# The position bias's rows to DRAM: one transfer from a borrowed tile, or eight from a tile of their own

## The chip, the cores and the metric

The kernel runs on one core of one Trainium2 chip. Its time is the device time of one execution, in microseconds (us). Engines are named as in the profile: PE multiplies, PEld loads its weights, ACT and DVE do elementwise work, POOL and SP here mostly issue DMA transfers. A transfer is cut into packets that run on the core's 16 DMA engines, whoever issued it.

## The reference

Two layers of a decoder trunk on 512 tokens of width 2048, in float32. Each layer normalises its input, projects it once, and runs two groups of attention heads on the result: eight heads of differential attention (two softmax maps a head) and eight heads of latent attention (low-rank queries, keys and values, a shared rotary key). Both are gated, joined and projected back.

Only the differential heads use the position bias: 32 buckets by 8 heads, one table for both layers.

```python
dist = (start + jnp.arange(BLOCK_Q, dtype=jnp.int32))[:, None] - kpos[None, :]
bias = jnp.transpose(table[_t5_bucket(dist)], (2, 0, 1))
s = jnp.where((dist >= 0)[None, None, None], s + bias[None, None], NEG_INF)
```

So the bias of a head is a function of the distance alone: one row of 640 numbers holds all of it (640 covers 512 keys and 128 query rows), and each query row reads that row at another offset.

## The kernel before

Activations lie feature-major, 128 features on the partitions and 512 tokens along a row. Every float32 operand of a matmul is split into a high and a low part, and each product is three matmuls (`mm3`). The weights come from DRAM as 290 blocks of 128 x 1024 numbers (512 KB, a few of half that). `WStream` handles them: SP issues the load of a block into one of two `raw` buffers (line 75), ACT casts it to `whi` (line 94), DVE subtracts to get `wlo` (line 95), and PE uses the pair. There are two buffers of each kind. The load of block i+2 can be issued only when DVE has finished with block i, so at most two loads are under way.

PE, SP and POOL execute in the order in which the program is written; the order on ACT and DVE is chosen by a scheduler. `run_jobs` sets the written order: jobs are generators of matmuls with a `yield` after every few, and a list of steps says after which yield each small piece of work is written down. A step sets a place in the order of the program. It makes an engine wait only if one of its instructions needs something that is not there yet.

The first layer begins with the compressed query (`job_kouter`), the rotary key (`job_kr`) and the compressed keys and values (four `job_proj`). In step 34 of these, `bias_rows` (line 823) multiplies the table with a one-hot matrix: PE writes an 8 x 640 result, DVE copies it to `tv` (line 832), and POOL issues one transfer that writes each of the eight rows 128 times to the DRAM tensor `brow` (line 833). The source pattern has 8 partitions, then a step of 0 with a count of 128, then 640 numbers. `tv` borrows the one buffer of tag `pth`, which the heads' transposed probabilities use later (`new_pt`).

After that come the eight units of latent attention (in the first layer and then in the second), each with its own jobs and `mla_steps`, and then the eight units of differential attention. At the start of each of these, `load_bias` (line 838) reads one head's bias from `brow` with a row step of 639, which gives each partition its own offset.

## Time and profile before

| | us |
|---|---|
| median of 3 runs | 1840.79 (1840.78 to 1840.84) |
| profiled execution, its own time | 1841.41 |
| its span in the trace | 1839.6 |
| PE busy | 1795.7 (98% of the span) |
| DVE busy | 1021.9 (56%) |
| ACT busy | 878.8 (48%) |
| POOL busy | 38.0 (2%) |

How to read it: the span is what the trace covers, and the execution's own time has 1.8 us more around it. PE is busy nearly all the time, so what is left to gain or lose lies in the few stretches in which PE stands still or runs at a lower clock, and in the work itself.

## The change

The 8 x 640 result gets a tile of its own, so the buffer of tag `pth` is no longer borrowed. The single transfer is removed from `bias_rows`. In its place the new function `bias_out` issues the transfer of one head's row, and a step at place 2 of each of the first layer's eight units of latent attention calls it. The number of bytes is the same.

```diff
-        tv = t_([NH, 640], F32, "pth", 1)
+        tv = sb.tile([NH, 640], F32, name="tv")
         for o, n in ((0, 512), (512, 128)):
             ps = p_("tp", 2)
             nc.tensor.matmul(ps[:NH, :n], tab, st["onehot"][:, o:o + n], start=True, stop=True)
             nc.vector.tensor_copy(out=tv[:, o:o + n], in_=ps[:NH, :n])
-        nc.gpsimd.dma_start(out=brow, in_=bass.AP(tensor=tv.tensor, offset=tv.offset, ap=[list(tv.ap[0]), [0, P], [1, 640]]))
+        st["tv"] = tv
+
+    def bias_out(hd):
+
+        row = st["tv"][hd:hd + 1, :]
+        nc.gpsimd.dma_start(out=brow[hd:hd + 1], in_=bass.AP(tensor=row.tensor, offset=row.offset, ap=[list(row.ap[0]), [0, P], [1, 640]]))
...
-            add(jobs, mla_steps(h, keep(8 + h), after(MLA_AT if h else FIRST_AT, sum(n for n, _ in jobs))))
+            add(jobs, mla_steps(h, keep(8 + h), after(MLA_AT if h else FIRST_AT, sum(n for n, _ in jobs))),
+                [(2, lambda h=h: bias_out(h))] if l == 0 else [])
```

The order of POOL's instructions from the start of the program, before the change, with the semaphores that each waits for (`DVE` counts DVE's instructions, `DMASW` the landings of POOL's own transfers, `DMAHW` those of SP's):

```order
masks.py:197 MEMSET ident 128x128
masks.py:199 ISA
masks.py:199 AFFINE_SELECT ident<-ident 128x128 [waits Pool_49]
L833 DMA brow<-pth_748 1024x1x640 [waits DVE_49]
L838 DMA cs_2933<-brow 128x512 [waits DMAHW6_49,DMASW0_49,DVE_49]
L838 DMA cs_2935<-brow 128x512 [waits DMAHW7_49,DVE_49]
```

And of the changed kernel, where line 838 is the transfer in `bias_out` and line 843 the load in `load_bias`:

```order
masks.py:197 MEMSET ident 128x128
masks.py:199 ISA
masks.py:199 AFFINE_SELECT ident<-ident 128x128 [waits Pool_49]
L838 DMA brow<-tv 128x1x640 [waits DVE_49]
L838 DMA brow<-tv 128x1x640 x7
L843 DMA cs_2940<-brow 128x512 [waits DMAHW6_49,DMASW0_49,DVE_49]
L843 DMA cs_2942<-brow 128x512 [waits DMAHW7_49,DMASW1_49,DVE_49]
```

One issue of 1024 rows has become eight of 128 rows that follow each other; the first waits for DVE, the other seven wait for nothing.

On ACT, in the first unit of latent attention, before the change (line 678 casts the transposed probabilities to `pth`, line 434 the values):

```order
L719 ACTIVATE sa_1139<-sa_1139,m_1140 128x256
L434 CAST v_1090<-pacc_1086 128x512
L434 CAST v_1090<-po_1087 128x512
L434 CAST v_1090<-pacc_1088 128x512
L434 CAST v_1090<-pacc_1089 128x512
L94 CAST whi_1208<-raw_1145 128x1024
```

The same place in the changed kernel:

```order
L678 CAST pth_1157<-ptp_1159 128x128
L719 ACTIVATE sa_1139<-sa_1139,m_1140 128x256
L434 CAST v_1089<-pacc_1085 128x512
L434 CAST v_1089<-po_1086 128x512
L678 CAST pth_1157<-ptp_1179 128x2x128
L434 CAST v_1089<-pacc_1087 128x512
L434 CAST v_1089<-pacc_1088 128x512
L94 CAST whi_1208<-raw_1145 128x1024
```

The first two casts to `pth` have moved ahead of the values' casts; before the change they stood some ten instructions later, behind a wait for the transfer of `brow`. DVE's subtractions that follow them (line 679) move likewise. SP's order is unchanged, and PE's too.

## Rows read from the trace of the kernel before

**Rows 1.** The page: its first line, and three DMA issues (KB each, us to landing).

```profile
span 1839.6 us, 21822 instructions
...
raw<-in_blocks_dram SPq DMA_DIRECT2D x282, 512.0 KB, 3.5
...
brow<-pth POOLq DMA_DIRECT2D x1, 2560.0 KB, 56.6
...
xres<-tmp POOLq DMA_DIRECT2D x8, 256.0 KB, 2.3
```

**Rows 2.** Waits of PE from 80 to 150 us: total, times, longest.

```profile
PE ptp L312 <- ACT sa L307: 15.8, 1, 15.8
PE pacc L319 <- ACT whi L94: 11.5, 1, 11.5
PE pacc L321 <- DVE wlo L95: 0.4, 1, 0.4
```

**Rows 3.** The chain of waits from 88 to 146 us: start, us, what.

```profile
89.14 23.86 DMA raw<-in_blocks_dram
113.09 1.05 ACT whi L94
114.17 1.23 DVE wlo L95
115.42 23.81 DMA raw<-in_blocks_dram
139.33 1.05 ACT whi L94
140.41 1.23 DVE wlo L95
142.94 0.80 PE ptp L312
```

**Rows 4.** Busy time of engines in four stretches, then granted clock, DMA share, GB/s.

```profile
102.70:114.10 11.40, 0.00 (x0) 0.00 (x0) 0.00 (x0) 1.01 (x2) 0.00 (x0) 0.60 0.49 76
114.20:118.60 4.40, 4.36 (x9) 2.97 (x10) 1.79 (x2) 0.47 (x1) 0.00 (x0) 0.50 0.73 146
127.20:142.80 15.60, 0.00 (x0) 0.00 (x0) 1.83 (x2) 2.10 (x3) 0.00 (x0) 0.66 0.50 75
143.00:149.30 6.30, 6.30 (x14) 4.69 (x15) 4.14 (x6) 5.53 (x10) 0.00 (x0) 0.50 0.16 58
```

**Rows 5.** PE in order of time, before and after the first standstill: start, us.

```profile
101.81 0.39 PE L319 MATMUL pacc<-x,whi 128*128 128x512 f32 x1
102.03 0.39 PE L320 MATMUL pacc<-x,whi 128*128 128x512 f32 x1
...
116.47 0.63 PE L320 MATMUL pacc<-x,whi 128*128 128x512 f32 x1
116.89 0.63 PE L321 MATMUL pacc<-x,wlo 128*128 128x512 f32 x1
```

**Rows 6.** POOL in order of time from 80 to 360 us.

```profile
87.50 1.23 POOL L833 DMA_DIRECT2D brow<-pth  x1 [86.20 <-DVE pth L832]
317.83 1.12 POOL L838 DMA_DIRECT2D cs<-brow  x2 [229.09 <-DVE tmp L578]
356.19 0.54 POOL L838 DMA_DIRECT2D cs<-brow  x1 [37.24 <-DVE m L663]
```

**Rows 7.** DMA queues from 98.5 to 104 us: packets, MB, share of 16 engines.

```profile
q0 software_dynamic: 52, 0.27, 47.4%
```

**Rows 8.** DMA queues from 105 to 111 us.

```profile
q0 software_dynamic: 55, 0.28, 40.4%
q1 hardware_dynamic: 56, 0.23, 9.3%
```

**Rows 9.** DMA queues from 432 to 434 us, one block's load alone.

```profile
q1 hardware_dynamic: 139, 0.52, 76.5%
```

**Rows 10.** Loads of blocks issued from 85 to 146 us.

```profile
DMA to landing us min/median/max: 3.3/21.2/26.8
```

**Rows 11.** ACT in order of time: casts of weight blocks.

```profile
91.58 1.05 ACT L94 CAST whi<-raw 128x1024 fp32r<-128x1024 f32 x1 [3.06 <-PE pacc L320]
113.09 1.04 ACT L94 CAST whi<-raw 128x1024 fp32r<-128x1024 f32 x1 [20.46 <-DMA raw<-in_blocks_dram]
120.79 1.05 ACT L94 CAST whi<-raw 128x1024 fp32r<-128x1024 f32 x1 [6.12 <-DMA raw<-in_blocks_dram]
139.33 1.04 ACT L94 CAST whi<-raw 128x1024 fp32r<-128x1024 f32 x1 [17.49 <-DMA raw<-in_blocks_dram]
```

**Rows 12.** Instructions on `pth` from 100 to 200 us: the casts (ns, starts).

```profile
L678 ACT CAST pth<-ptp x6: 255/378/587, 180.4 to 198.7; 128x128 fp32r<-128x128 f32 x2, 128x256 fp32r<-128x256 f32 x2, 128x384 fp32r<-128x384 f32 x1, 128x512 fp32r<-128x512 f32 x1
```

**Rows 13.** Waits of PE from 150 to 450 us.

```profile
PE ptp L672 <- DVE ptl L679: 0.4, 1, 0.4
```

## What the change will do to the time

> **What bounds the kernel now.** I read the page first: PE is the bound, so I looked for the places where PE stands still. Of the waits of PE, three lie between 80 and 150 us and make 27.7 us: 11.5, 15.8 and 0.4 [rows 2]. The chain of waits says what stands behind the two long ones: a load of a weight block that took 23.9 us from issue to landing, and a second one of 23.8 us [rows 3]; ACT's casts at 113.1, 120.8 and 139.3 us all waited for such loads, where the one at 91.6 still waited for PE [rows 11]. Over the whole run such a load of 512 KB takes 3.5 us in the median [rows 1]. The only other thing under way is the transfer that writes the bias rows: 2560 KB, issued at 87.50 us, landed 56.6 us later, at 144.1 [rows 1, 6]. Loads issued in that time took up to 26.8 us, and the one issued as it ended took 3.3 again [rows 10].

> The standstills also cost clock. [...] At 0.50 a matmul starts every 0.42 to 0.43 us, at full clock every 0.22 to 0.23 [rows 5], so 23 matmuls lost some 0.2 us each: 4.6 us. In all the bias transfer costs the kernel 27.7 + 4.6 = 32.3 us. This is the most that any placing of it can win.

> **What the change does to the transfer.** It does not spread it. POOL executes in the order written, and a step only sets a place in that order. In the changed program the eight issues stand directly behind each other, the first waits for DVE's copy and the other seven for nothing. POOL is idle from 88.7 to 317.8 us [rows 6], so nothing else there holds them apart. An issue of 128 rows keeps POOL 0.54 us against 1.23 for the 1024 rows [rows 6]: eight make 4.3 us, and all are issued from 87.5 to about 91.8 us. I cost POOL's added 3.1 us at nothing: its next work comes at 317.8. So the same 2560 KB meet the same loads, and the question is how fast they move and which engines they keep.

> How fast they move now, from a stretch with no load in it: 52 packets in 5.5 us, 0.27 MB, 47.4% of 16 engines [rows 7]. That is 7.6 engines at work, so eight, one for each source row; 0.27 MB / 5.5 us = 49 GB/s; and 0.474 x 16 x 5.5 / 52 = 0.80 us for a packet of 0.27 MB / 52 = 5.2 KB (two rows of 2560 B). Where a load runs between them, its packets of 4 KB take 0.093 x 16 x 6 / 56 = 0.16 us, 25.7 GB/s on one engine [rows 8]. At that rate 5.12 KB would take 0.199 us; the bias packets take 4.03 times as long, as if four engines took turns at something that passes what one engine can move. The same rows show that it is not the engines that are full: with 9.3% given to the load, the bias still moved 55 packets in 6 us, 9.2 a us against 9.5, and each took only 0.404 x 16 x 6 / 55 = 0.71 us. So the eight rows have two such bottlenecks between them, each 25.7 GB/s, 51 together; this I take to lie on the reading side, four neighbouring partitions to one.

> [...]

> After the change each transfer reads one partition 128 times. **Which engines** carry it is not in the trace of before. A transfer of 128 rows runs on all 16: a load alone kept 76.5% of them busy in 2 us [rows 9]. One whose source had 8 partitions ran on eight. The new one has one partition and 128 repeats. The bounds are one engine and sixteen; I take sixteen, since both its sides count 128 rows, as the load does. [...]

> With sixteen engines at one bottleneck of 25.7 GB/s, 2.62 MB need 102 us instead of the 53.4 us at 49 GB/s. Adding the 3 us around it (56.6 - 53.4), the bias ends at about 87.5 + 3 + 102 = 192.5 us instead of 144.1. Rows 0 to 3 go through one bottleneck first and rows 4 to 7 through the other after them, since the transfers stand in line on the same engines.

> **What PE gets meanwhile.** A packet now takes 16 x 0.199 = 3.2 us on every engine. Of a load, each engine has 128 / 16 = 8 packets. Now a load takes 23.9 - 3.5 = 20.4 us longer, about 25 bias packets of 0.80 us, 8 of them in turn with its own and some 17 ahead of them. After the change an engine has 32 bias packets in all. The load issued at 89.14 finds those of three or four transfers ahead (12 to 16) and takes turns with 8 more: 20 to 24 packets, so it lands at 89 + 2 + 64 to 77 = 155 to 168, not at 113. The next (issued at 93.92) takes turns with the following 8 and lands near 183. The third can only be issued when the first is split; it lands with the end of the bias, about 192.5, not at 139.2. In the chain of before PE starts again 142.94 - 139.23 = 3.7 us after that landing [rows 3], so at 196 instead of 142.9: +53. The lower end is plain turn-taking with nothing ahead (8 x 3.2 us for each load): landings at 116, 142, 168 and 193, PE waiting for the fourth then and one block of work (24 matmuls of 0.227, 5.4 us) further than in the other case: +47. Lower clock is lost in either case after two or three standstills, as now, give or take 3 us. The upper end: both loads under way stay behind the whole bias to 192.5, so PE restarts at 194 with two blocks still to do (7.6 us with the low clock, 5.4 us without) and is at the third block at 207 instead of 142.9, with no standstill before it (-2.8 us): +61. I take +49, between the two that share turns.

> **The rest of the change.** The first two casts to `pth` and their subtractions stand earlier, since they no longer wait for the bias. They ran at 180 us [rows 12], after the transfer had landed at 144.1, so that wait had ended anyway. What may go is the one wait of PE for a subtraction, 0.4 us [rows 13]; what may come is a delay of a weight cast by two casts of 0.26 and 0.38 us: -0.4 to +0.6, taken as 0. A small reordering on DVE in the first differential unit is of the same size. If the bias lasts to 192.5, the borrowed tile would have held these casts at 180 back; with a tile of its own it does not, so this part of the change is a cover and no gain.

> **Sum.** 1841.4 + 49 = 1890.4; the profiled execution lies 0.6 above the median of 1840.8, so 1890. The likeliest case's own range is 1870 to 1912: +45 to +61, and some more at either end for a bottleneck that passes 5% more or 10% less (102 us x 0.1 = 10).

> **The rivals.**
> - One engine carries all eight transfers (faster). It would have the bottleneck to itself, 0.199 us a packet, for 102 us. A load's packets there wait 25 x 0.199 = 5.0 us, so it lands after 8.5 us. The load issued at 89.14 was needed when PE ran dry at 102.7 less 1.2 us for the cast [rows 3, 4], so 12 us are to spare and PE never stops: 1841.4 - 32.3 = 1809, up to 1818 if a few loads with less room come late. For it: a source with 8 partitions ran on eight engines, and this one has one. Against it: the 128 repeats on both sides.
> - The 49 GB/s belong to the transfer's queue or to all eight rows, and sixteen engines or eight change nothing in the sum: it ends at 144 as before. The first load lands at about 125 instead of 113 (a packet takes 1.6 us on 16 engines), and what PE loses there it gets back at the third, whose load now lands before it is needed: 1838 to 1848. Against it: the factor of 4.03 fits a count of four.
> - Each engine has its own 6.4 GB/s on such rows (5.12 KB / 0.80 us), and sixteen make 102 GB/s: the bias ends at 116, the second standstill of 15.8 us and its 2.8 us of clock go, 1822. Against it: the packets of 0.71 us [rows 8].
> - One partition can be read at 6.4 GB/s only: 410 us of bias, some 350 us slower. Against it: a transfer of 256 KB out of 128 partitions lands after 2.3 us, 16 KB an engine, over 7.1 GB/s each [rows 1].

> **How the numbers follow.** The likeliest case 0.66; one engine 0.13; the sum unchanged 0.11; 6.4 GB/s an engine 0.05; far slower, by this or another way, 0.05. For 8 times in 10 the range goes from 1818 to 1912: the first case, the unchanged sum, 6.4 GB/s an engine, and the edge of one engine. About 0.2% (3.7 us) can be told from no change. Faster: 0.13 + 0.05 and 0.02 of the unchanged sum, 0.20. Within: 0.07. Slower: 0.66 + 0.05 + 0.02 = 0.73.

> **What the profile of the changed kernel would show.** POOL: eight issues of about 0.54 us from 87.5 to 92 us; were they 20 us or more apart, the first step is wrong. DMA: in the stretch without loads 16 engines near full and about 26 GB/s; half of them and 49 GB/s, or one engine (6% and 26 GB/s), means a rival. Landing of the last bias row near 192 us. PE: a standstill of 50 to 65 us from 102.7, and one or two shorter ones before 196; none at all would mean that one engine carries it. From 200 us on nothing should differ by more than 1 us.

## The result, and the profile after

The changed kernel took 1890.15 us (median of four runs, 1887.34 to 1890.85) against 1840.78 of before (1840.64 to 1840.84), measured beside it: a ratio of 1.0266, interval 1.0251 to 1.0282. The execution that was profiled is the lowest of the four, 1887.34 us.

The page of the kernel after: its span, PE busy in 40 slices, and the line of the bias transfers (KB each, us to landing), to be read against [rows 1].

```profile
span 1885.6 us, 21827 instructions
...
PE   9922999999999999999999999999999999999997
...
brow<-tv POOLq DMA_DIRECT2D x8, 320.0 KB, 54.6
```

A slice is 47 us, so nearly all of the damage lies between 94 and 189 us. POOL in order of time from 80 to 360 us (start, us, what, how often) shows that the eight transfers were not spread:

```profile
87.07 4.28 POOL L838 DMA_DIRECT2D brow<-tv  x8 [85.77 <-DVE tv L832]
```

The same line's landings, all eight: 87.1 + 14.4 = 101.5 us for the first, 90.8 + 91.6 = 182.4 for the last, where the one transfer of before had landed at 144.1.

```profile
L838 POOL DMA_DIRECT2D brow<-tv x8: 522/524/663, 87.1 to 90.8; - x8
...
DMA to landing us min/median/max: 14.4/54.6/91.6
```

The DMA queues from 96 to 136 us (packets, MB, share of 16 engines; POOL's queue, then SP's), which answer [rows 7, 8]:

```profile
q0 software_dynamic: 263, 1.09, 90.6%
q1 hardware_dynamic: 176, 0.66, 4.0%
```

All 16 engines are kept by the bias, and together they move 1.09 MB in 40 us, 27 GB/s, where eight moved 49 before. A busy engine here is one that is held up: in experiment 3 the same queue moves 262 GB/s at a share of 73.6%. What the loads beside it pay stands in the chain of waits from 88 to 188 us, as in [rows 3]:

```profile
88.71 47.74 DMA raw<-in_blocks_dram
136.55 1.05 ACT whi L94
137.63 1.24 DVE wlo L95
138.88 44.81 DMA raw<-in_blocks_dram
183.80 1.05 ACT whi L94
184.87 1.23 DVE wlo L95
...
187.40 0.79 PE ptp L312
```

47.7 and 44.8 us for a load that took 23.9 and 23.8 before, and PE starts again at 187.40, not at 142.94. The load between these two, issued at 93.5 us, took longest. Loads of blocks issued from 85 to 160 us, to be read against [rows 10]:

```profile
DMA to landing us min/median/max: 3.5/38.5/59.8
```

The waits of PE from 80 to 700 us (total, times, longest), as in [rows 2, 13]:

```profile
PE pacc L319 <- ACT whi L94: 44.5, 2, 35.4
PE ptp L312 <- ACT sa L307: 26.3, 1, 26.3
PE ps L754 <- DVE m L663: 2.4, 1, 2.4
```

The first line holds two standstills, 35.4 and 9.1 us. And the stretches, as in [rows 4] (busy time of PE, PEld, DVE, ACT and POOL, granted clock, DMA share, GB/s): the longest standstill, and what follows each of the three.

```profile
102.30:137.50 35.20, 0.00 (x0) 0.00 (x0) 0.00 (x0) 0.95 (x1) 0.00 (x0) 0.57 0.99 52
137.70:141.50 3.80, 3.76 (x8) 2.56 (x9) 1.75 (x2) 0.43 (x1) 0.00 (x0) 0.50 0.89 43
...
154.60:158.60 4.00, 3.96 (x9) 2.66 (x10) 1.74 (x2) 0.00 (x0) 0.00 (x0) 0.50 0.86 24
...
187.40:192.70 5.30, 5.30 (x12) 3.90 (x13) 3.14 (x5) 4.55 (x8) 0.00 (x0) 0.50 0.11 42
```

After each of the three standstills PE runs 8, 9 and 12 matmuls at a granted clock of 0.50, 29 in all against 9 + 14 = 23 before [rows 4].

The difference of the two profiled executions, 1887.34 - 1841.41 = 45.9 us, comes out of these rows: standstills 35.4 + 9.1 + 26.3 = 70.8 against 27.7, +43.1; six more matmuls at 0.50, 0.2 us each [rows 5], +1.2; the new wait at L754, +2.4; a start 0.4 us earlier (POOL's issue at 87.07, not 87.50) and the wait of 0.4 at L672 that is gone, -0.8. Sum: +45.9. The medians lie 49.4 apart: the profiled execution of after is the fastest of its four and lies 2.8 below their median, while that of before lies 0.6 above its own. What makes the other executions of after some 3 us longer no trace here shows.

## The experiments

The theory: what holds the loads up is the reading of the bias rows. Few partitions are read through one bottleneck of some 26 GB/s (25.7 by the estimate from [rows 8], 27 measured in the kernel after), and the engines that carry them are held up with it. After the change all sixteen stand at one such bottleneck at a time. Rivals: the tile, the queue, the number of bytes written, the number of engines.

**1. The tile alone** (before, with the new tile and the single transfer).

```diff
-        tv = t_([NH, 640], F32, "pth", 1)
+        tv = sb.tile([NH, 640], F32, name="tv")
```

> One transfer of eight rows as before the change, but from a tile of its own. Theory (the loss comes from eight transfers that each read one partition): 1840.8, within 1 us of before, the transfer lands after 56 to 57 us and PE's standstills stay 11.5 and 15.8 us. Rival (the tile of its own, or the reordering of the casts that it brings, costs the time): 1880 or more.

1840.11 us against 1840.66, ratio 0.9997 (0.9988 to 1.0006). The waits of PE and the landing of the bias are those of before:

```profile
PE ptp L312 <- ACT sa L307: 15.8, 1, 15.8
PE pacc L319 <- ACT whi L94: 11.5, 1, 11.5
...
DMA to landing us min/median/max: 56.5/56.5/56.5
```

The tile, with the reordering of the casts that it brings, costs and gives nothing; the 49 us belong to the eight transfers and the steps that issue them.

**2. Eight rows from partitions four apart** (before, with the table's columns repeated four times, so that a matmul makes 32 rows; the one transfer reads partitions 0, 4, ... 28).

```diff
...
+        wide = st["wide"]
+        nc.vector.tensor_copy(out=wide.rearrange("k (h r) -> k h r", r=4), in_=bass.AP(tensor=tab.tensor, offset=tab.offset, ap=[list(tab.ap[0]), [1, NH], [0, 4]]))
-        tv = t_([NH, 640], F32, "pth", 1)
+        tv = t_([4 * NH, 640], F32, "pth", 1)
...
-        nc.gpsimd.dma_start(out=brow, in_=bass.AP(tensor=tv.tensor, offset=tv.offset, ap=[list(tv.ap[0]), [0, P], [1, 640]]))
+        nc.gpsimd.dma_start(out=brow, in_=bass.AP(tensor=tv.tensor, offset=tv.offset, ap=[[4 * tv.ap[0][0], NH], [0, P], [1, 640]]))
```

> One transfer of eight rows as before, from the borrowed tile, but the rows lie on partitions 0, 4, 8 to 28 instead of 0 to 7 (the table's columns are repeated four times, so the matmul makes 32 rows). Same engines, same bytes. Theory (four neighbouring partitions share one bottleneck of 25 to 27 GB/s): each engine has one to itself, a packet takes 0.2 us, the transfer lands 15 to 17 us after its issue, no load takes over 10 us, PE has no standstill of over 1 us, 1808 to 1813. Rival (49 GB/s belong to the transfer's queue, or 6.4 GB/s to each engine on rows that are read again): lands after 56 us as before, 1841.

1808.47 us, ratio 0.9824 (0.9809 to 0.9839). Bytes, queue and count of source rows are unchanged, and only their distance is new. The landing of the bias, then the DMA queues from 99.5 to 104.5 us:

```profile
DMA to landing us min/median/max: 19.9/19.9/19.9
...
q0 software_dynamic: 178, 0.91, 43.6%
```

0.91 MB in 5 us, 182 GB/s, from the same number of engines as in [rows 7] (43.6% and 47.4%), against 49 GB/s. The bottleneck lies on the reading side, in where the rows stand. The landing missed its expected 15 to 17 by 3 us.

**3. The rows in all 128 partitions** (before, each column repeated 16 times; every partition is read eight times).

```diff
...
+        nc.vector.tensor_copy(out=wide.rearrange("k (h r) -> k h r", r=16), in_=bass.AP(tensor=tab.tensor, offset=tab.offset, ap=[list(tab.ap[0]), [1, NH], [0, 16]]))
...
+        nc.gpsimd.dma_start(out=brow.rearrange("h (a r) t -> (h a) r t", r=NH), in_=bass.AP(tensor=tv.tensor, offset=tv.offset, ap=[list(tv.ap[0]), [0, NH], [1, 640]]))
```

> One transfer, but the matmul makes each head's row on sixteen partitions (128 in all), and each partition is read eight times instead of 128. Theory: sixteen engines with sixteen bottlenecks, 2.62 MB at 16 x 25.7 GB/s in 6.4 us, lands 8 to 11 us after its issue, no standstill of PE over 1 us, 1807 to 1812. Rival (writing to DRAM or the queue limits): lands after 25 us or more and PE stands still for 5 us or more, 1815 to 1841.

1807.86 us, ratio 0.9822 (0.9808 to 0.9835), the lowest median of all kernels run here (those of experiments 2 and 6 lie within 1.1 us of it). The landing of the bias, the DMA queues from 89 to 99 us, and, apart, the only wait of PE that is left from 80 to 450 us:

```profile
DMA to landing us min/median/max: 10.8/10.8/10.8
...
q0 software_dynamic: 528, 2.62, 73.6%
q1 hardware_dynamic: 234, 0.88, 21.5%
```

```profile
PE pacc L321 <- DVE wlo L95: 0.2, 1, 0.2
```

The whole 2.62 MB went in 10 us, 262 GB/s, on 16 engines, with 0.88 MB of loads beside it (3.4 to 8.5 us to landing). It landed after 10.8 us, within the 8 to 11 expected. Work on sixteen engines did no harm here, where none was held up.

**4. Eight transfers, the halves in turn** (after, issued in the order 0, 4, 1, 5, 2, 6, 3, 7).

```diff
-                [(2, lambda h=h: bias_out(h))] if l == 0 else [])
+                [(2, lambda h=h: bias_out(h // 2 + 4 * (h % 2)))] if l == 0 else [])
```

> The changed kernel with its eight transfers in the order 0, 4, 1, 5, 2, 6, 3, 7, so that neighbours in the line read from the two groups of four partitions in turn. Theory (the engines go through the line in step, one transfer at a time, and overlap by a packet where the group changes; in the changed kernel the landings are 12 us apart, 9.9 and 8.6 where the group or the line ends): seven overlaps of 2 to 3 us instead of one, so the last row lands some 12 to 18 us earlier than at 182, 1870 to 1882. Rival (the line does not matter, both groups are used in full side by side): the last row lands near 140, 1840 to 1850. Rival (the limit is one for all rows): no change, 1888 to 1891.

1852.97 us, ratio 1.0065 (1.0052 to 1.0079): 37 us faster than after, and lower than the 1870 to 1882 expected. The line of the issues and the landings:

```profile
L838 POOL DMA_DIRECT2D brow<-tv x8: 522/523/666, 86.8 to 90.6; - x8
...
DMA to landing us min/median/max: 13.7/41.4/57.2
```

The last lands at 90.6 + 57.2 = 147.8, 61 us after the first issue: 43 GB/s, much nearer to two bottlenecks side by side (49) than to one (27). The expected overlap of about a packet a neighbour was too small. The first two transfers still land one after the other (100.5 and 113.5 us), but the third and the fourth, which read from different groups, land 36.2 and 37.3 us after issues 0.5 us apart, where the third and fourth of after landed 39.3 and 48.6 us after theirs: they were under way at once. That some engines had run a transfer ahead of others is the reading that fits; that each engine held packets of two transfers would fit too, and no run tells the two apart.

**5. Really spread** (after, with a copy of one element of the unit's key tile on POOL ahead of each issue, so that the issue waits for that unit).

```diff
+        touch = t_([1, 1], F32, "touch", 1)
+        nc.gpsimd.tensor_copy(out=touch, in_=f32(st["k"][0:1, 0, 0:1]))
```

> The changed kernel, but ahead of each of the eight issues POOL copies one number of the keys of that unit, so that the issue waits for its unit: the spreading that the written order alone doesn't give. Theory: the eight issues stand 15 to 30 us apart from 150 us on, each transfer still takes 12 us on all 16 engines, and a load that meets one lands after 10 to 16 us instead of 3.5; PE's standstills before 150 us go (-32 us) and up to eight short ones of 0 to 5 us come: 1809 to 1850, most likely 1820. Rival (it is the bytes that cost, wherever they lie): 1885 or more. Rival (the spreading hides all): 1809, no standstill over 1 us.

1816.74 us, ratio 0.9873 (0.9858 to 0.9888). POOL in order of time, the first two of eight; then the loads of blocks issued from 125 to 330 us; then the waits of PE from 80 to 450 us:

```profile
128.66 0.17 POOL L838 COPY touch<-ka 1x1 f32<-1x1 f32 x1 [127.36 <-ACT ka L543]
128.91 0.66 POOL L840 DMA_DIRECT2D brow<-tv  x1
149.67 0.17 POOL L838 COPY touch<-ka 1x1 f32<-1x1 f32 x1 [20.10 <-ACT ka L543]
149.79 0.53 POOL L840 DMA_DIRECT2D brow<-tv  x1
```

```profile
DMA to landing us min/median/max: 2.6/3.6/14.0
```

```profile
PE ptp L672 <- ACT sa L719: 3.4, 1, 3.4
PE ps L754 <- DVE m L663: 2.4, 1, 2.4
PE pacc L319 <- DVE tmp L578: 1.1, 3, 0.4
```

Each transfer still goes through one bottleneck (13.8 us in the median), and a load that meets it takes up to 14.0, but PE has that much to spare: the time is within the 1809 to 1850 expected. So it wasn't the idea of spreading that cost 49 us: the change didn't spread. Of the 8.9 us to experiment 3, these waits hold 6.9; what made the 3.4 was not followed.

**6. Eight transfers back to back, from 16 partitions each** (rows as in experiment 3).

```diff
...
+        for hd in range(NH):
+            row = tv[16 * hd:16 * hd + 16, :]
+            nc.gpsimd.dma_start(out=brow[hd].rearrange("(a r) t -> a r t", r=NH), in_=bass.AP(tensor=row.tensor, offset=row.offset, ap=[list(row.ap[0]), [0, NH], [1, 640]]))
```

> Eight transfers issued back to back as in the changed kernel, with the same rows and bytes each, but each reads its head's row from sixteen partitions (eight times each) instead of one (128 times). Theory: it is not the count of transfers but the one partition; sixteen partitions make four groups, 4 x 25.7 = 103 GB/s or more, the eight land within 26 to 29 us of the first issue, the first load lands near 110 instead of 136, and PE stands still once, for 5 to 10 us: 1812 to 1825. Rival (eight transfers in line on 16 engines are what delays the loads): the landings as in the changed kernel, 1885 to 1891.

1808.93 us, ratio 0.9829 (0.9813 to 0.9846). PE's longest wait from 80 to 450 us is 0.4.

```profile
DMA to landing us min/median/max: 5.2/11.9/15.2
```

Eight issues from POOL, 2560 KB and 6000 packets on POOL's queue over the run, as after, and no harm. The count of transfers is cleared. The last landed 18.9 us after the first issue, not 26 to 29 as expected, and the standstill of 5 to 10 us that was expected didn't come.

**7. Eight transfers back to back, one row each, four partitions apart** (rows as in experiment 2).

```diff
...
+        for hd in range(NH):
+            row = tv[4 * hd:4 * hd + 1, :]
+            nc.gpsimd.dma_start(out=brow[hd:hd + 1], in_=bass.AP(tensor=row.tensor, offset=row.offset, ap=[list(row.ap[0]), [0, P], [1, 640]]))
```

> Eight transfers back to back, each reading one partition 128 times as in the changed kernel, but the rows lie on partitions 0, 4, 8 to 28, each in a group of four of its own (borrowed tile, 32 rows from the matmul). Theory after the run with alternating rows (the engines don't go through the line in step: an engine that is done with its share of a row starts the next, and where that lies in another group it moves at its full 0.2 us a packet): the rows overlap strongly, the last lands 25 to 45 us after the first issue instead of 95, 1812 to 1832. Rival (one partition at a time, in step): 12 us a row as in the changed kernel, 1885 to 1891.

1829.03 us, ratio 0.9933 (0.9916 to 0.9949). The waits of PE and the landings (of the slowest of its four executions, 1834.29 us):

```profile
PE pacc L319 <- ACT whi L94: 16.2, 1, 16.2
PE ptp L312 <- ACT sa L307: 4.0, 1, 4.0
...
DMA to landing us min/median/max: 13.9/33.5/38.5
```

On POOL's queue this is after (6000 packets over the run in both) with one thing changed: the eight rows lie four partitions apart, as those that passed 182 GB/s in experiment 2. It is 61 us faster (2.4 of it the wait at L754, which it lacks). The bias ends 42 us after the first issue, not 95, and both this and the time lie within what was expected: transfers in line from rows four apart overlap by more than half, but not as one transfer that reads them all does (19.9).

**8. Four rows in partitions 0 to 3 and four in 32 to 35, two transfers** (before; the matmul makes 36 rows, and those between hold zeros).

```diff
...
+        nc.vector.tensor_copy(out=wide[:, 0:4], in_=tab[:, 0:4])
+        nc.vector.tensor_copy(out=wide[:, 32:36], in_=tab[:, 4:8])
...
+        for hd in (0, 4):
+            rows = tv[8 * hd:8 * hd + 4, :]
+            nc.gpsimd.dma_start(out=brow[hd:hd + 4], in_=bass.AP(tensor=rows.tensor, offset=rows.offset, ap=[list(rows.ap[0]), [0, P], [1, 640]]))
```

> Two transfers of four rows, the first four on partitions 0 to 3, the others on 32 to 35 instead of 4 to 7 (borrowed tile). Theory (a bottleneck belongs to four neighbouring partitions): two of them, each transfer passes 25 to 27 GB/s, and on engines of their own both end after 53 to 57 us as in the kernel before, 1838 to 1845. [...]

1883.33 us, ratio 1.0231 (1.0216 to 1.0247). Landings, then the DMA queues from 98.5 to 125 us, then PE's waits from 80 to 450, then the loads of blocks issued from 85 to 146:

```profile
DMA to landing us min/median/max: 100.9/101.1/101.3
...
q0 software_dynamic: 139, 0.71, 47.9%
```

```profile
PE pacc L319 <- ACT whi L94: 33.6, 3, 27.7
PE ptp L312 <- ACT sa L307: 26.4, 1, 26.4
```

```profile
DMA to landing us min/median/max: 3.7/40.1/49.3
```

Two transfers on eight engines (47.9%), under way together, move 0.71 MB in 26.5 us: 27 GB/s, as one partition at a time in after, against 49 for rows 0 to 7 [rows 7]. So the rows in partitions 0 to 3 and those in 32 to 35 were held up at one bottleneck here, and the theory that one belongs to four neighbours alone is wrong: by it the time would have been 1838 to 1845. The kernel answers a second question too: half of the engines are free, and the loads are nearly as late as with all sixteen held up. In the median and at most they take 40.1 and 49.3 us, against 47.7 and 59.8 in after from the same stretch, and these two waits of PE make 60.0 us against 70.8. That fits a load that is spread over all 16 engines [rows 9] and lands with the slowest of them; the trace does not show the engines one by one.

## Why the prediction was right, and where its terms were off

The time was right (1890 predicted), and so was the mechanism; three sizes were off, in ways that partly cancel. That the median came out within 1 us is therefore in part luck.

- **It does not spread the transfer.** Right: one row of POOL holds all eight issues, within 4.28 us. Experiment 5 shows what a wait in front of each does.
- **Sixteen engines at one bottleneck.** Right: 90.6% of 16 engines and 27 GB/s. The rivals (one engine, the sum unchanged, 6.4 GB/s an engine, far slower) are excluded by these two numbers. Experiments 2 and 7 show that the place of the rows is the cause.
- **The rate.** Taken as 25.7 GB/s from a load's packets on one engine [rows 8]; measured 27, and a little more where rows 3 and 4 overlap. The seven landings after the first took 182.4 - 101.5 = 80.9 us, 28 packets of each engine (320 KB a transfer, in packets of two rows as in [rows 7] four an engine; from 90 to 102 us some 62 such packets carry 0.32 MB, 5.2 KB each), 2.9 us a packet and not 3.2. The bias ended at 182.4, not at 192.5.
- **The first load.** Predicted to land at 155 to 168, with 12 to 16 packets ahead of it and 8 in turn; it landed at 88.71 + 47.74 = 136.5. (47.7 - 3.5) / 2.9 is about 15 packets and not 20 to 24: if the engines take turns packet by packet, 8 came in turn and some 7 stood ahead, so the queue ahead was taken about twice too long. From 90 to 102 us SP's queue moved one packet while the bias moved 0.32 MB, four packets an engine, so some did stand ahead; the split of the 15 is not measured. The second load landed at 153.3 (93.5 + 59.8), not near 183. The third landed at 183.7, with the end of the bias as the step said, and PE restarted at 187.4: +44.5 over before, not +53, and below the low end of +47 too, which rested on 3.2 us a packet. The sign that was named for PE, a standstill of 50 to 65 us from 102.7, did not come: with the first two loads early, PE stood still for 35.4, 9.1 and 26.3 us.
- **The reordering on DVE, taken as 0.** Wrong: 2.4 us at L754. DVE from 426 us on in the kernel after, and the same place in the kernel before:

```profile
426.50 0.69 DVE L653 TENSOR_TENSOR mb<-tmp,mb 64x512 fp32r<-64x512 f32 x1
430.78 1.23 DVE L95 TENSOR_TENSOR wlo<-raw,whi 128x1024 fp32r<-128x1024 f32 x1 [3.59 <-ACT whi L94]
431.92 0.28 DVE L663 CUSTOM_DVE_ANT_0 sa<-ps,cs 128x128 f32<-128x128 f32 x1
```

```profile
383.34 0.69 DVE L653 TENSOR_TENSOR mb<-tmp,mb 64x512 fp32r<-64x512 f32 x1
385.18 0.29 DVE L663 CUSTOM_DVE_ANT_0 sa<-ps,cs 128x128 f32<-128x128 f32 x1 [1.15 <-PE ps L756]
...
387.85 1.22 DVE L95 TENSOR_TENSOR wlo<-raw,whi 128x1024 fp32r<-128x1024 f32 x1
```

  The split of a weight block now stands ahead of the scores' mask on DVE; it waits 3.59 us for ACT's cast, and the mask behind it, and PE behind the mask, wait with it. "From 200 us on nothing should differ by more than 1 us" was wrong by this. The wait is in the trace of after and of experiments 4 and 5, which issue the transfers as steps of the units, and in none of the others: it comes with those steps, and not with the tile alone, which experiment 1 has too.
- **The clock.** Taken as equal; +1.2 us from a third standstill, inside the 3 us allowed.
- **The limit of 32.3 us** that any placing can win: experiments 2, 3 and 6 took 31.5 to 32.8 us off.
- **The range.** Its low end of 1870 does not follow from its terms: 1841 + 45 less 5% of 102 us is 1881. The result lies inside either.

For the profiled execution the sum was thus 3 us high: the loads were over-priced and DVE under-priced. The median hides this, since it lies 2.8 us above that execution.

## What to carry to other kernels

A step in this schedule set only an order: the seven issues that waited for nothing went out behind the first, all eight within 4.28 us, and only with a wait on the work that each was to follow (experiment 5) did they stand apart, the first two by 20.9 us. A broadcast that reads one or a few neighbouring partitions many times held up every DMA engine it was spread on here, and the loads beside it (one partition at a time on sixteen engines: 27 GB/s at 90.6% busy, loads of up to 59.8 us; eight neighbours on eight: 49 GB/s at 47.4%, loads of up to 26.8 [rows 7, 10]). With the rows written into all partitions first, here by repeating columns ahead of a matmul, the same bytes landed in a fifth of the time (10.8 us against 56.6); rows four partitions apart did as well for the kernel's time (1808.47 us against 1807.86). Look at the rate beside the busy share: the engines that were 90% busy at 27 GB/s were waiting for one source.

- The bias moved at 27 GB/s both when one partition was read at a time (the kernel after) and when eight that stand 0 to 3 and 32 to 35 were read together (experiment 8, 101 us for 2.62 MB). Eight at 0 to 7 got 49 GB/s [rows 7]; eight that are four apart got 182 with a load beside them (experiment 2).
- Transfers issued back to back overlapped by far more than a packet when each read from another group of four partitions than the one ahead of it: with rows 0 to 3 and 4 to 7 in turn 2.62 MB took 61 us (experiment 4), with eight rows four partitions apart 42 (experiment 7), against about 95 with 0 to 3 and then 4 to 7 (the kernel after). What lets them overlap is not shown.
- Halving the number of engines that are held up helped the loads little: they took up to 49.3 us with eight held up (experiment 8) and up to 59.8 with sixteen (the kernel after).
